# LRU gates placed inside the pair loop, 64x64 prompt scores, late scaling and a reordered start in a two-group encoder layer

## The chip, the cores and the metric

The kernel runs on one core of one Trainium2 chip. The metric is the device time in microseconds of one execution. Lower is better.

## What is computed

One layer of a streaming encoder, for 512 prompt tokens and 8 x 16 sample tokens that share all weights (`D` = 1024). Everything is float32. Cut to what matters here:

```python
def layer_forward(x, p, lb, cache, win_rows):
    x = x + 0.5 * swiglu(rms_norm(x, p['norm_ffn1']), p['w_ffn1_up'], p['w_ffn1_down'])   # D_FF = 2816
    m, st = mixer(rms_norm(x, p['norm_mix']), p, lb, cache, win_rows)
    x = x + m
    x = x + 0.5 * swiglu(rms_norm(x, p['norm_ffn2']), p['w_ffn2_up'], p['w_ffn2_down'])
    return x, st
# mixer: (aq, ak, av, hq, hf, hi, hg, lx, lg, ga, gb, gc) = split(h @ w_in)
#   A: attention, 16 heads in 4 groups, q and k normed per head; a prompt chunk of 64 queries
#      sees its own chunk and the two before it (192 keys); one learned sink per head
#   B: HGRN2, a gated linear recurrence
#   C: xc = conv4(lx);  r = sigmoid(xc @ lru_w_a + b_a);  ig = sigmoid(xc @ lru_w_x + b_x)
#      log_a = -8 * r * softplus(-lambda);  a = exp(log_a)
#      h_t = a_t * h_(t-1) + sqrt(1 - a_t^2) * ig_t * xc_t;   yc = h * gelu(lg)
#   merged = sigmoid(ga)*(ya@w_attn_o) + sigmoid(gb)*(yb@w_hgrn_o) + sigmoid(gc)*(yc@w_lru_o);  out = merged @ w_out
```

## The kernel before

**Layout.** Activations lie with features on the 128 partitions and the 640 tokens (512 prompt, then 128 sample) along the free axis, so x is eight tiles of 128x640. The matmul inputs are split into a high and a low part in a rounded float32 type (fp32r): `RA` and `RB` hold eight high tiles (0 to 7) and eight low tiles (8 to 15). `proj(w, r0, nk, c0, R)` makes one 128-column output tile of a weight: it loads the weight tile `wr` (512 KB, three buffers), makes `wh` and `wl` from it (lines 750 and 751), and issues for each of `nk` row blocks three products (wh x high, wh x low, wl x high) on two halves of 320 tokens, six matmuls a row block and 48 for eight. The result stands in two `pp` buffers of PSUM out of four, so that at most two projections are open. `scaled` moves it out, times the norm's factor `RS` (`late=False`), or copies it first and multiplies later (`late=True`).

**Order of the work.** The program is first recorded as a list of operations and then emitted by a planner, `Sched.run`, which keeps one in-order list for each engine. At each step it takes the operation that can start first by its own clock; among those that can start within 0.04 us of the earliest, the lowest priority number goes first. The priority is the number of the projection, `S.item`, plus `S.late`, or `S.item` less `lag` for loads and weight splits. Durations come from formulas: `dve(n)` is 0.066 + 1.042e-3 * n us, and `mm` has a `cost` for each kind of tile, with `RESIZE` = 0.1 us where the width of the output changes. Buffers come from tags (`pp` 4, `me` 2, `ml` 2 in PSUM; `wr`, `wh`, `wl`, `qq`, `lg`, `mgC` and more in SBUF), and the buffers of a tag are handed out strictly in program order. On the chip each engine follows its list and waits where an input isn't there.

**Stages,** with the stretches of the profiled span they fill:
- *Start (0 to 32 us).* `load_x` loads x in quarters (four prompt loads of 512 KB and four sample loads of 128 KB) through SP's queue; the first weight tile stands behind the first quarter. PE transposes each quarter, ACT and DVE copy it and split it into `RA`; ACT squares it for the first norm. `lag` in `load_x` orders the loads.
- *FFN 1 (to 470).* The hidden width is done in chunks of 4, 6, 6 and 6 tiles. The first chunk uses `proj`, the rest a Strassen-like scheme, `pair`, whose operands `combos` makes. Half of these are made by the function `rest()` that it returns, called ahead of the first chunk's down projections. *FFN 2 (1482 to the end)* is the same code with `sfx` "2". In FFN 1 the first two tiles are scaled late, in FFN 2 none.
- *Attention (470 to 700).* `qknorm` norms queries and keys; `query(m)` writes two heads (m of 8) as `qb`, 1024 columns, in which each head's block has zeros in the other head's rows. `prompt(m)` takes the 8 chunks of 64 queries in two halves `hh`, in each of which it makes two groups `i` of two chunks: one 128x128 by 64-to-192-column matmul for each chunk into a `me` buffer, a maximum (line 1064), exponentials, sums, then transposes (`pT`) and the product with the values (`pv_of`). `AHEAD` says how many gate or branch projections follow each m.
- *LRU (767 to 890).* `lru()` has a loop over four pairs of tiles: convolution of `branch(m)` (the first four are made in attention), two small projections with the block-diagonal weights `BH`/`BL` by `NH`/`NL`, exponentials, a scan along the tokens (line 1227), and the gate branch `LG`. Its end rows go to `CB` by copies that POOL or DVE may take. After the loop come five projections of the merge gate `GC`, `heads(0)` and `merge`.
- *HGRN2 (1010 to 1335)*, then `w_out` and FFN 2.

Of the kernel before, what the change touches and what calls it, by code (L numbers as in the profile page):

```python
# [345 lines left out]
def trunk_kernel(ctx: ExitStack, tc: tile.TileContext, A: dict, O: list):  # L346
# [122 lines left out]
    SK = fixed("SK", [P, 32])  # L469
    NAR = 13864  # L470
# [52 lines left out]
    in_region(RW, 2, [("qb", 1024, 2), ("pw", 1024, 2)])  # L523
# [23 lines left out]
    fill(EPSC.v, EPS, only=("DVE",))  # L547
    fill(ONEF[0:64, 64:128], 0.0, only=("DVE",))
# [195 lines left out]
    def proj(w, r0, nk, c0, R):  # L744
# [4 lines left out]
        dma(r, w[r0:r0 + nk * P, c0:c0 + P].rearrange("(k p) f -> p k f", p=P), lag=4)  # L749
        S.op([act(nk * P, lambda: nc.scalar.copy(h(), r())), dve(nk * P * 0.5, lambda: nc.vector.tensor_copy(h(), r()))], [r], [h], lag=2)  # L750
        S.op([dve(nk * P, lambda: nc.vector.tensor_tensor(l(), r(), h().bitcast(F32), op=ALU.subtract))], [r, h], [l], lag=1.5)  # L751
        ps = [S.buf("pp") for _ in range(2)]
        for k in range(nk):
            mm([(ps[i][:, :HT], a[:, k, :], R[:, o + k, i * HT:(i + 1) * HT].at(o + k), k == 0 and j == 0, k == nk - 1 and j == 2)
                for j, (a, o) in enumerate(((wh, 0), (wh, 8), (wl, 0))) for i in range(2)])
# [216 lines left out]
    def attention():  # L972
        ck, cv = A["cache_attn_k"][0], A["cache_attn_v"][0]
        sk = A["attn_sinks"][0].rearrange("(m two) -> two m", two=2)
        for h in range(2):
            dma(SK[h * 64:h * 64 + 64, 0:8].at(h), sk[h:h + 1, :].to_broadcast([64, 8]), after=(PRM.v,), small=True)
            for b in range(4):
                p0 = b * 32 + h * 16
                dma(SK[p0:p0 + 16, 8:16].at((b, h)), sk[h:h + 1, :].to_broadcast([16, 8]), after=(PRM.v,), small=True)
        S.op([dve(16, lambda: nc.vector.tensor_scalar(SK[:, 16:32](), SK[:, 0:16](), -1.0, None, op0=ALU.mult))], [SK.v, RS.v], [SK.v])  # L980
# [23 lines left out]
        for j in range(2):  # L1004
            q, r = qknorm(proj(W, 0, KD, AK + j * P, RA))
# [35 lines left out]
        def prompt(m, g, qb):  # L1041
            pT = S.buf("pT")
            for hh in range(2):
# [4 lines left out]
                for i in range(2):  # L1048
                    ps = S.buf("me")
                    calls = []  # L1050
                    for c in (2 * i, 2 * i + 1):
                        n = hh * 4 + c
                        w = min(n + 1, 3) * 64
                        o = (c % 2) * 192
                        e = 192 if c % 2 == 0 else 256
                        win[c] = ps[:, o:o + w], pw3[:, c, e - w:e].at(c)
                        calls.append((win[c][0], qb[:, n * P:(n + 1) * P], kd[g][:, (n + 1) * 64 - w:(n + 1) * 64], True, True))
                    mm(calls)
                    if hh == 0 and i == 0:
                        red = [(mx[:, c:c + 1].at(i), win[c][0]) for c in range(2)]  # L1060
# [5 lines left out]
                    ts(mi, mi, -0.125, ALU.mult, SK[:, 16 + m:17 + m], ALU.min, only=("DVE",))  # L1066
                    fn(ei, mi, AF.Exp, bias=SK[:, m:m + 1])
                    for c in (2 * i, 2 * i + 1):
                        fn(win[c][1], win[c][0], AF.Exp, scale=0.125, bias=mx[:, c:c + 1].at(i), accum=den[:, c:c + 1].at(i))
                    tt(di, di, ei, ALU.add, only=("DVE",))  # L1070
                    recip(di, di)
                    for c in (2 * i, 2 * i + 1):
                        ts(win[c][1], win[c][1], den[:, c:c + 1].at(i), ALU.mult)
# [8 lines left out]
            def pv_of(k, n):  # L1082

                src = pT[:, k * 512:k * 512 + n * 256].r("p (c h q) -> p c h q", h=2, q=64)
                mm([(po[h * 64:h * 64 + 64, k * P:(k + n) * P].r("p (c q) -> p c q", q=64), V[:, k, g, :], src[:, :, h, :], k == 0, k == 3)
                    for h in range(2)])
# [82 lines left out]
    def lru():  # L1169
        bds = [S.buf("bd") for _ in range(2)]  # L1170
        for b in bds:
            fill(b.v, 0.0)
        for j in range(4):
            xcs, rs, igs, las, lts = [], [], [], [], []
            for i in range(2):
# [16 lines left out]
                cp(CB[:, m, 0:3].at(m), y[:, TP - 3:TP], only=("POOL", "DVE"))  # L1192
                cp(CB[:, m, 3:27].at(m).r("p (b j) -> p b j", b=NB), smp(y.v)[:, :, SB - 3:], only=("POOL", "DVE"))
# [294 lines left out]
```

## Time and profile before

| | |
|---|---|
| median of 3 runs | 1921.0 us (1920.73 to 1923.34) |
| the profiled execution | 1923.28 us, span 1921.5 us, mean granted TensorE clock 0.996 |
| PE busy | 1898.9 us in 14654 instructions |
| PEld (weight loads beside PE) | 1853.0 us |
| DVE busy | 1389.1 us |
| ACT busy | 735.8 us |
| POOL busy | 44.3 us |
| HBM read and written | 143.32 and 10.63 MB |

Times are from the start of the span. A matmul's duration in the profile runs to the modelled end of its result, so a following matmul starts before it: the step from one start to the next says what an instruction costs in a stream, and busy time is the union of such spans. A float32 matmul call is two PE instructions in the profile, an fp32r one is one. `RA`, `RB` and the other names are the program's; most SBUF tiles outside them are slices of one tensor, `AR`, and are named so in the profile.

### The profile page before, as it was taken

What the parts mean: (1) busy time and instruction counts of PE and PEld (TensorE: products, weight loads), DVE (VectorE), ACT (ScalarE), POOL (GpSimd) and SP (SyncE); (2) the same over time, 40 slices, a digit from 0 to 9 for tenths busy, and PEclk for the clock granted to TensorE, in tenths of its full rate; (3) what the DMA queues carried; (4) which work ended last, traced back from release to release, by engine and by line L of the source; (5) the groups of instructions that cost most, each with busy time, mean ns of one, the idle gap of its engine ahead of it and who ended that gap; (6) DMA issues with size and microseconds to landing.
All of it is one profiled execution on the core that took longest, in us unless ns stands there. A gap on an engine that the chain in (4) does not pass through costs nothing.

```text
span 1921.5 us, 35215 instructions
## 1 busy us (share of the span) xinstructions
PE 1898.9 (99%) x14654; PEld 1853.0 (96%) x14654; DVE 1389.1 (72%) x2599; ACT 735.8 (38%) x1295; POOL 44.3 (2%) x86
## 2 busy tenths in 40 slices
PE   8999999999999999999999999999999999999999
PEld 8999999999999999999999999999999999999998
DVE  7897685877787773787547778877556978586784
ACT  6343251433478630876002344335112324142340
POOL 2000000000000000020000000000000000000000
PEclk9999999999999999999999999999999999999999
DMA  6232332224321212213222222222322133222322
GB/s 144 66 94 80 93 87 78 75 78 139 102 62 50 62 48 77 61 57 103 77 77 74 84 80 79 79 81 83 122 72 77 56 99 90 87 65 79 99 64 80
DMA packets 303488, 156.89 MB, mean 82 GB/s; under 512 B 21324, under 2 KB 300956, under 8 KB 303328
## 3 DMA queue, kind: packets, MB, share of 16 engines
q1 hardware_dynamic: 302576, 154.58, 27.7%
q8 instruction: 115, 1.88, 0.4%
q0 software_dynamic: 736, 0.06, 0.4%
q14 instruction: 45, 0.37, 0.1%
q10 hardware_dynamic: 16, 0.00, 0.0%
HBM read 143.32 MB, written 10.63 MB: 80 GB/s over the span
## 4 chain that ended last, share of the span: by engine, by line
PE 93%; DVE 4%; ACT 2%; issue 1%; DMA 1%; SPq 0%; ACTq 0%; DVEq 0%
PE pp L438 84%; PE me L438 4%; PE ml L438 3%; PE ml L447 1%; PE me L447 1%; DVE AR L383 1%; ACT AR L393 1%; DVE AR L369 1%; DVE RB L369 0%; DVE AR L1227 0%; ACT L393 0%; DMA RX<-in_x_prompt_dram 0%; DVE wl L751 0%; SPq L417 0%; DVE RA L369 0%
## 5 line engine op out<-in xcount | busy, mean ns | idle before, releaser
L438 PE MATMUL pp<-RA,wh 128*128 128x320 f32 x4192 | 815.0, 314 | 0.3 <-DVE AR L369 0.3
L438 PEld LDWEIGHTS pp<-RA,wh 128*128 128x128 f32 x4192 | 659.1, 189 | 13.1 <-issue 9.7
L438 PE MATMUL pp<-RA,wl 128*128 128x320 f32 x2096 | 490.7, 310 | 4.9 <-DVE wl L751 4.9
L438 PE MATMUL pp<-RB,wh 128*128 128x320 f32 x2016 | 389.0, 310 | 0.9 <-DVE AR L369 0.9
L438 PEld LDWEIGHTS pp<-RA,wl 128*128 128x128 f32 x2096 | 354.7, 188 | 5.9 <-DVE wl L751 5.9
L438 PEld LDWEIGHTS pp<-RB,wh 128*128 128x128 f32 x2016 | 320.4, 188 | 1.5 <-DVE AR L369 1.4
L750 DVE CAST wh<-wr 128x1024 fp32r<-128x1024 f32 (+2 forms) x142 | 89.4, 630 | 237.2 <-PE pp L438 236.5
L438 PE MATMUL pp<-RB,wl 128*128 128x320 f32 x1008 | 241.9, 310 | 1.6 <-DVE wl L751 1.6
L751 DVE TENSOR_TENSOR wl<-wr,wh 128x1024 fp32r<-128x1024 f32 (+2 forms) x196 | 216.7, 1106 | 1.6 <-ACT wh L750 1.0
L836 ACT CAST RW<-AR 128x512 fp32r<-128x512 f32 x180 | 110.4, 621 | 264.9 <-PE pp L438 135.0
L438 PEld LDWEIGHTS pp<-RB,wl 128*128 128x128 f32 x1008 | 172.1, 188 | 1.9 <-DVE wl L751 1.9
L369 DVE TENSOR_TENSOR AR<-AR 128x640 f32<-128x640 f32 (+12 forms) x272 | 140.0, 519 | 28.9 <-ACT AR L393 16.5
L369 DVE TENSOR_TENSOR AR<-pp,AR 128x320 f32<-128x320 f32 x268 | 127.6, 485 | 35.8 <-PE pp L438 32.7
L393 ACT ACTIVATE AR<-AR 128x640 f32<-128x640 f32 (+2 forms) x184 | 110.5, 604 | 96.9 <-DVE AR L369 89.6
L438 PE MATMUL pp<-RX,RW 128*128 128x320 f32 x864 | 138.6, 309 | 0.0
L438 PEld LDWEIGHTS pp<-RX,RW 128*128 128x128 f32 x864 | 129.6, 188 | 0.0
L833 DVE TENSOR_TENSOR RW<-AR,RW 128x512 fp32r<-128x512 f32 x180 | 122.3, 686 | 2.4 <-ACT RW L836 0.9
L393 ACT ACT_TABLE_LOAD x73 | 93.7, 1283 | 2.5 <-PEq L1476 1.4
L402 ACT COPY AR<-me 128x512 f32<-128x512 f32 (+3 forms) x72 | 25.8, 373 | 123.9 <-PE me L447 115.2
L383 DVE SCALAR_TENSOR_TENSOR AR<-pp,AR 128x320 f32<-128x320 f32 x128 | 61.3, 483 | 15.5 <-PE pp L438 15.4
L438 PE MATMUL pp<-RY,RW 128*128 128x320 f32 x432 | 69.2, 309 | 0.0
L750 ACT CAST wh<-wr 128x1024 fp32r<-128x1024 f32 (+1 forms) x54 | 53.7, 994 | 36.9 <-PE pp L438 36.5
(195 smaller groups left out, 1960.7 us busy)
## 6 DMA issues: line engine op xcount, KB each, us to landing
wr<-in_w_in_dram SPq DMA_DIRECT2D x84, 512.0 KB, 3.7
wr<-in_w_ffn_up_dram SPq DMA_DIRECT2D x52, 512.0 KB, 3.8
AR<-in_w_ffn_up_dram SPq DMA_DIRECT2D x36, 512.0 KB, 4.6
wr<-in_w_ffn_down_dram SPq DMA_DIRECT2D x48, 384.0 KB, 3.3
wr<-in_w_ffn_down_dram SPq DMA_DIRECT2D x16, 256.0 KB, 2.8
wr<-in_w_attn_o_dram SPq DMA_DIRECT2D x8, 512.0 KB, 3.7
AR<-in_state_hgrn_dram SPq DMA_DIRECT2D x8, 512.0 KB, 4.7
wr<-in_w_lru_o_dram SPq DMA_DIRECT2D x8, 512.0 KB, 3.8
```

The costliest lines, as they stand in the source:

```text
L369: alts = [dve(out.n, lambda: nc.vector.tensor_tensor(out(), a(), b(), op=op))]
L383: return S.op([dve(out.n, lambda: nc.vector.scalar_tensor_tensor(out(), a(), ap_of(s), b(), op0=op0, op1=op1), isinstance(s, View))], [a, ...
L393: nc.scalar.activation(out(), a(), func, bias=ap_of(bias), scale=ap_of(scale), **kw)
L402: alts = [act(out.n, lambda: nc.scalar.copy(out(), a()), 0, a), dve(out.n * (1.0 if a.in_psum else 0.5), lambda: nc.vector.tensor_copy(out ...
L438: nc.tensor.matmul(o(), l(), m(), start=s, stop=e)
L447: nc.tensor.transpose(o(), i(), d())
L750: S.op([act(nk * P, lambda: nc.scalar.copy(h(), r())), dve(nk * P * 0.5, lambda: nc.vector.tensor_copy(h(), r()))], [r], [h], lag=2)
L751: S.op([dve(nk * P, lambda: nc.vector.tensor_tensor(l(), r(), h().bitcast(F32), op=ALU.subtract))], [r, h], [l], lag=1.5)
L833: S.op([dve(out.n, lambda: nc.vector.tensor_tensor(out(), a(), b(), op=op))], [a, b], [out], lag=lag)
L836: S.op([act(out.n, lambda: nc.scalar.copy(out(), a()))], [a], [out], lag=lag)
```

## The change

- *Start:* 14 matmuls of 128x128 on the constant `ONEF` are recorded ahead of x. The first weight tile is loaded and split in four pieces of two row blocks, each ordered behind a quarter of x by its lag; the lags of x's quarters change a little.
- *FFN:* `rest()` gets `S.late` = 4. In FFN 2 the first tile is now scaled late.
- *Attention:* `qb` is a plain 512 columns, written by one operation over all partitions. The scores of a half `hh` are one group of eight calls on 64x64 tiles: for each chunk and head a tile with 64 rows and 64 output partitions, placed so that two chunks fill all four quarters of the array; even chunks go to one `me` buffer and odd ones to the other. For odd chunks the heads stand in swapped halves, for which the sinks `SK` get swapped copies and `pv_of` reads other columns. The key projections are scaled late.
- *LRU:* one of the `GC` gates is projected inside each of the four pairs and the fifth after them. The planner's duration of the scan is doubled. The copies into `CB` go to ACT or DVE.
- *HGRN2:* the copies of the 16-blocks go to ACT or DVE.

```diff
@@ mm, cost
+            if l.proto.shape[0] == 64 and w == 64:
+                return max(0.054, 0.42e-3 * m.n)
@@ buffers
-    SK = fixed("SK", [P, 32])
+    SK = fixed("SK", [P, 48])
-    in_region(RW, 2, [("qb", 1024, 2), ("pw", 1024, 2)])
+    in_region(RW, 2, [("qb", 512, 2), ("pw", 1024, 2)])
@@ start
+    warm = S.buf("me")
+    mm([(warm[:, i % 4 * P:(i % 4 + 1) * P], ONEF.v, ONEF.v, True, True) for i in range(14)])
@@ load_x
-            lag = (12, 2.7, 2.6, 2.5)[c]
+            lag = (12, 2.7, 2.65, 2.6)[c]
@@ proj
-    def proj(w, r0, nk, c0, R):
+    def proj(w, r0, nk, c0, R, slices=None):
...
+        if slices is not None:
+            for k in range(0, nk, 2):
+                rk, hk, lk = (b[:, k:k + 2, :].at(k) for b in (wr, wh, wl))
+                dma(rk, src[:, k:k + 2, :], lag=slices[k // 2])
+                cp(hk, rk, only=("ACT", "DVE"))
+                tt(lk, rk, hk.cast(F32), ALU.subtract)
@@ ffn
-                    late = not sfx and f < 2
-                    g = scaled("fA" + sfx, proj(wu, 0, KD, f * P, R), late)
+                    late = f < (1 if sfx else 2)
+                    g = scaled("fA" + sfx, proj(wu, 0, KD, f * P, R, (13, 3.69, 3.64, 3.59) if not sfx and f == 0 else None), late)
...
             if f0 == 0:
+                S.late = 4.0
                 rest()
+                S.late = 0.0
@@ attention
+            dma(SK[64 - h * 64:128 - h * 64, 32:40].at((h, 8)), sk[h:h + 1, :].to_broadcast([64, 8]), after=(PRM.v,), small=True)
...
-        for b in qbs + qss + pws:
+        for b in qss + pws:
             fill(b.v, 0.0, only=("POOL",))
...
-            q, r = qknorm(proj(W, 0, KD, AK + j * P, RA))
+            q, r = qknorm(proj(W, 0, KD, AK + j * P, RA), True)
@@ prompt
-                for i in range(2):
-                    ps = S.buf("me")
-                    calls = []
-                    for c in (2 * i, 2 * i + 1):
...
-                        calls.append((win[c][0], qb[:, n * P:(n + 1) * P], kd[g][:, (n + 1) * 64 - w:(n + 1) * 64], True, True))
-                    mm(calls)
+                pss, calls = [S.buf("me") for _ in range(2)], []
+                for c in range(4):
...
+                    o = (c // 2) * 192
+                    win[c] = pss[c % 2][:, o:o + w], pw3[:, c, e - w:e].at(c)
+                    for f in range(2):
+                        a, b = f * 64, (f ^ (c % 2)) * 64
+                        calls.append((win[c][0][a:a + 64, :], qb[b:b + 64, n * 64:(n + 1) * 64], kd[g][b:b + 64, (n + 1) * 64 - w:(n + 1) * 64],
+                                      True, True))
+                mm(calls)
@@ query
+            stt(qb.v, q[:, 0:TP], prm(QN), r[:, 0:TP], ALU.mult, ALU.mult)
             for h in range(2):
-                stt(qb[a:b, :].at(h).r("p (n h q) -> p n h q", n=8, h=2)[:, :, h, :], q[a:b, 0:TP].r("p (n q) -> p n q", n=8), prm(QN, a, b),
-                    r[a:b, 0:TP].r("p (n q) -> p n q", n=8), ALU.mult, ALU.mult)
@@ lru
+        gates, more = [], lambda m: gate(GC, m, "mgC")
...
-                cp(CB[:, m, 0:3].at(m), y[:, TP - 3:TP], only=("POOL", "DVE"))
+                cp(CB[:, m, 0:3].at(m), y[:, TP - 3:TP], only=("ACT", "DVE"))
...
-                S.op([dve(T, lambda o=hs.v, a=a.v, t=t.v: nc.vector.tensor_tensor_scan(o(), a(), t(), 0.0, op0=ALU.mult, op1=ALU.add))],
+                S.op([dve(2 * T, lambda o=hs.v, a=a.v, t=t.v: nc.vector.tensor_tensor_scan(o(), a(), t(), 0.0, op0=ALU.mult, op1=ALU.add))],
...
                 parts(RB, m, g.v)
+                if i == 0:
+                    gates.append(more(len(gates)))
...
-        more = lambda m: gate(GC, m, "mgC")
-        gates = [more(m) for m in range(5)]
+        while len(gates) < 5:
+            gates.append(more(len(gates)))
@@ hgrn
-                            cp(a4[p, :, p].at(j), atc[p, :].r("p (t l) -> p t l", t=NT), only=("ACT", "POOL"))
+                            cp(a4[p, :, p].at(j), atc[p, :].r("p (t l) -> p t l", t=NT), only=("ACT", "DVE"))
```

More of the change, by code (lines that the diff above doesn't have):

```diff
@@ L979, in attention @@
                 dma(SK[p0:p0 + 16, 8:16].at((b, h)), sk[h:h + 1, :].to_broadcast([16, 8]), after=(PRM.v,), small=True)
-        S.op([dve(16, lambda: nc.vector.tensor_scalar(SK[:, 16:32](), SK[:, 0:16](), -1.0, None, op0=ALU.mult))], [SK.v, RS.v], [SK.v])
+        for o, c, n in ((16, 0, 16), (40, 32, 8)):
+            S.op([dve(16, lambda o=o, c=c, n=n: nc.vector.tensor_scalar(SK[:, o:o + n](), SK[:, c:c + n](), -1.0, None, op0=ALU.mult))],
+                 [SK.v, RS.v], [SK.v])
         ms = S.buf("ms")
@@ L993, in attention, with qknorm @@
         qbs, qss, pws = ([S.buf(t) for _ in range(2)] for t in ("qb", "qs", "pw"))
-        for b in qbs + qss + pws:
+        for b in qss + pws:
             fill(b.v, 0.0, only=("POOL",))
-        def qknorm(ps):
-            q, s, r, u = scaled("qq", ps), S.buf("qt"), S.buf("qr"), S.buf("qu")
+        def qknorm(ps, late=False):
+            q, s, r, u = scaled("qq", ps, late), S.buf("qt"), S.buf("qr"), S.buf("qu")
             rnorm(q, s, r, u, bd64, 64)
@@ L1047, in prompt @@
                 win = {}
-                for i in range(2):
-                    ps = S.buf("me")
-                    calls = []
-                    for c in (2 * i, 2 * i + 1):
[L1052 to L1056, printed above, removed]
-                        calls.append((win[c][0], qb[:, n * P:(n + 1) * P], kd[g][:, (n + 1) * 64 - w:(n + 1) * 64], True, True))
-                    mm(calls)
-                    if hh == 0 and i == 0:
-                        red = [(mx[:, c:c + 1].at(i), win[c][0]) for c in range(2)]
+                pss, calls = [S.buf("me") for _ in range(2)], []
+                for c in range(4):
+                    n = hh * 4 + c
+                    w = min(n + 1, 3) * 64
+                    o = (c // 2) * 192
+                    e = 192 if c % 2 == 0 else 256
+                    win[c] = pss[c % 2][:, o:o + w], pw3[:, c, e - w:e].at(c)
[4 more added lines that the diff above has]
+                mm(calls)
+                for i, ps in enumerate(pss):
+                    cols = [(2 * i, win[i]), (2 * i + 1, win[i + 2])]
+                    if hh == 0:
+                        red = [(mx[:, c:c + 1].at(i), v[0]) for c, v in cols]
                     else:
@@ L1065, in prompt @@
                     mi, di, ei = (x[:, 2 * i:2 * i + 2].at(i) for x in (mx, den, es))
[L1066 to L1069, printed above, removed]
+                    pos, neg = ((0, 16), (32, 40))[i]
+                    ts(mi, mi, -0.125, ALU.mult, SK[:, neg + m:neg + m + 1], ALU.min, only=("DVE",))
+                    fn(ei, mi, AF.Exp, bias=SK[:, pos + m:pos + m + 1])
+                    for c, v in cols:
+                        fn(v[1], v[0], AF.Exp, scale=0.125, bias=mx[:, c:c + 1].at(i), accum=den[:, c:c + 1].at(i))
                     tt(di, di, ei, ALU.add, only=("DVE",))
                     recip(di, di)
-                    for c in (2 * i, 2 * i + 1):
-                        ts(win[c][1], win[c][1], den[:, c:c + 1].at(i), ALU.mult)
+                    for c, v in cols:
+                        ts(v[1], v[1], den[:, c:c + 1].at(i), ALU.mult)
                 for i in range(2):
@@ L1082, in pv_of @@
             def pv_of(k, n):
-                src = pT[:, k * 512:k * 512 + n * 256].r("p (c h q) -> p c h q", h=2, q=64)
-                mm([(po[h * 64:h * 64 + 64, k * P:(k + n) * P].r("p (c q) -> p c q", q=64), V[:, k, g, :], src[:, :, h, :], k == 0, k == 3)
-                    for h in range(2)])
+                src = pT[:, k * 512:k * 512 + n * 256].r("p (t x q) -> p t x q", x=4, q=64)
+                mm([(po[h * 64:h * 64 + 64, k * P:(k + n) * P].r("p (t e q) -> p t e q", e=2, q=64), V[:, k, g, :],
+                     src[:, :, 1:3, :] if h else src[:, :, 0:4:3, :], k == 0, k == 3) for h in range(2)])
             for k, n in ((0, 2), (2, 2), (1, 2), (3, 1)):
@@ L1191, in lru @@
                     stt(smp(xc.v)[:, :, :s], hist, w, smp(xc.v)[:, :, :s], ALU.mult, ALU.add)
-                cp(CB[:, m, 0:3].at(m), y[:, TP - 3:TP], only=("POOL", "DVE"))
-                cp(CB[:, m, 3:27].at(m).r("p (b j) -> p b j", b=NB), smp(y.v)[:, :, SB - 3:], only=("POOL", "DVE"))
+                cp(CB[:, m, 0:3].at(m), y[:, TP - 3:TP], only=("ACT", "DVE"))
+                cp(CB[:, m, 3:27].at(m).r("p (b j) -> p b j", b=NB), smp(y.v)[:, :, SB - 3:], only=("ACT", "DVE"))
                 r, ig = S.buf("lr"), S.buf("li")
@@ L1226, in lru @@
                 hs = rs[i]
-                S.op([dve(T, lambda o=hs.v, a=a.v, t=t.v: nc.vector.tensor_tensor_scan(o(), a(), t(), 0.0, op0=ALU.mult, op1=ALU.add))],
+                S.op([dve(2 * T, lambda o=hs.v, a=a.v, t=t.v: nc.vector.tensor_tensor_scan(o(), a(), t(), 0.0, op0=ALU.mult, op1=ALU.add))],
                      [a.v, t.v], [hs.v])
-                cp(CB[:, m, 27:28].at(m), hs[:, TP - 1:TP], only=("POOL", "DVE"))
-                cp(CB[:, m, 28:36].at(m), smp(hs.v)[:, :, SB - 1], only=("POOL", "DVE"))
+                cp(CB[:, m, 27:28].at(m), hs[:, TP - 1:TP], only=("ACT", "DVE"))
+                cp(CB[:, m, 28:36].at(m), smp(hs.v)[:, :, SB - 1], only=("ACT", "DVE"))
                 hss.append(hs)
```

12 lines of the change are left out of this document (7 added, 5 removed).

## The prediction, made before the change was run

> **What bounds the kernel now.** I read the mean clock first (0.996 on the one core), then the first part of the page, then PE's list of waits, then windows of the stages, then the timeline at each stall.
>
> PE is busy 1898.9 us of a span of 1921.5, so nearly everything that isn't PE is already covered. Time can come from two places only: PE's own instructions, and the stretches in which PE waits or runs below its full pace. The second kind is found by counting matmuls in windows. In the first fence the columns are the window, its length, busy time with instructions in brackets for PE, PEld, DVE, ACT and POOL, then the granted clock. The row 144 to 192 is the full pace: 329 matmuls in 48 us, 6.854 per us or 0.146 us each. A window with fewer has lost the difference, through idle time or a low clock.
>
> ```profile
> core 0: us, PE busy (x) PEld busy (x) DVE busy (x) ACT busy (x) POOL busy (x), PEclk, DMA share, GB/s
> 9.45:14.50 5.05, 5.01 (x21) 5.04 (x22) 3.54 (x6) 4.12 (x12) 4.23 (x8) 1.00 1.13 323
> 76.00:90.00 14.00, 12.41 (x73) 11.99 (x72) 12.64 (x35) 3.15 (x5) 0.00 (x0) 0.88 0.20 57
> 144.00:192.00 48.00, 48.00 (x329) 48.00 (x328) 35.12 (x61) 16.85 (x29) 0.00 (x0) 1.00 0.28 81
> 513.00:700.00 187.00, 186.45 (x1520) 172.37 (x1519) 149.64 (x416) 133.95 (x338) 1.28 (x6) 1.00 0.21 57
> 788.00:800.00 12.00, 9.22 (x45) 8.33 (x44) 12.00 (x21) 9.46 (x13) 3.72 (x4) 0.74 0.11 31
> 820.00:830.00 10.00, 7.62 (x52) 7.36 (x51) 10.00 (x19) 3.41 (x5) 4.05 (x6) 1.00 0.22 64
> 1486.00:1500.00 14.00, 13.11 (x88) 12.63 (x87) 12.55 (x20) 2.15 (x3) 0.00 (x0) 1.00 0.13 39
> 1532.00:1550.00 18.00, 16.28 (x100) 15.88 (x99) 12.85 (x25) 1.47 (x3) 0.00 (x0) 0.91 0.20 58
> ```
>
> The waits say what PE stood for; columns are total us, times, longest.
>
> ```profile
> PE pp L438 <- DVE wl L751: 6.4, 5, 2.4
> PE me L447 <- DMA RX<-in_x_prompt_dram: 4.6, 2, 2.6
> PE me L438 <- DVE NL L369: 2.4, 1, 2.4
> PE ml L447 <- DMA AR<-in_norm_ffn_dram: 2.3, 1, 2.3
> PE pp L438 <- DVE AR L369: 1.2, 2, 0.9
> ```
>
> The reader is to see that each wait is for a small DVE operation standing behind others in DVE's queue, or for x at the start. In attention (513 to 700) PE loses only 0.55 us of 187: there the PE instructions themselves must go.
>
> **The change part by part.**
>
> *Prompt scores.* Before, each head pair m issues 8 calls of 128x128 weights, half of the query block being zeros; each call is two PE instructions. After: 16 calls of 64x64 on the four quarters of the array.
>
> ```profile
> 514.45 0.45 PE L438 MATMUL pp<-RA,wl 128*128 128x320 f32 x2
> 514.74 0.81 PE L438 MATMUL me<-AR,RW 128*128 128x192 f32 x4
> 515.26 0.88 PE L438 MATMUL pp<-RA,wh 128*128 128x320 f32 x4
> ...
> L438 PE MATMUL me<-AR,RW 128*128 128x192 f32 x96 | 19.6, 331 | 0.0
> ...
> L438 PE MATMUL ml<-AR 128*64 128x256 f32 x96 | 12.1, 388 | 0.0
> ...
> L438 PE MATMUL me<-AR 128*32 128x128 f32 x128 | 5.2, 279 | 0.0
> ```
>
> A group of four instructions of 192 columns holds PE from 514.74 to 515.26, 0.52 us, and the projection behind it needs 0.88 for its first four instead of the usual 0.75, 0.13 more: 0.65 us, so 163 ns per instruction. Per m there are three such groups and one of 64 and 128 columns, which I estimate from this at 0.55: 2.5 us, and 20.0 us for the eight m.
> After, what one instruction costs depends on how many quarters work at once. The trace has no 64x64 tile, but it has halves and strips. The 64-wide weights (x96, eight groups of twelve) take 12.1/8 = 1.51 us a group; less the 0.39 of the last one, starts are 1.12/11 = 102 ns apart, half of the 217 that 256 columns would take alone at 163 per 192: two at once. The 32-wide ones (x128, eight groups of 16) are (0.65 - 0.28)/15 = 25 ns apart against 109 alone: four at once. Both ways of cutting the array run at their full number, so I take four at once: 41 ns for 192 columns, and 27 ns for the short ones, estimated at the closest starts just found. Per m: 24 x 0.041 + 8 x 0.027 = 1.2 us, plus two groups (not four) that each pay 0.13 on return and 0.1 for the change of width, the planner's own constant: 1.66. Eight m: 13.3 us. Gain 6.7, say 7.0, as some old groups also stood apart by small gaps. Upper end 10 (20.0 less bare 1.2 x 8).
> A rule of the Trainium skill speaks against this. "TensorEngine Tiling (Array Packing)", Gotcha 1, says that different row tiles cannot use one PSUM bank at the same time, and here the first two calls (rows 0 to 63 and rows 64 to 127) write two halves of one bank. By that rule only two quarters would overlap and the sum would end at 1909.9; no run so far shows two row tiles on one bank, so it stands as a rival below.
> With two at once the scores cost 24 x 0.082 + 8 x 0.054 + 0.46 = 2.86 per m, 22.9 in all: 2.9 worse than now. That is the lower end.
> Beside it: one query operation over 128 partitions replaces two over 64, the zero fills go, and the first half's reductions become two in each bank; by the planner's 0.066 us start that is under 0.6 us of DVE in all, hidden, as DVE is busy 149.64 and ACT 133.95 of 187. If that cover were gone it would cost the 0.6. The scores now wait for both `me` buffers; see the rivals. The value matmuls only read other columns: 0. Two more small POOL loads of the sinks stand 500 us ahead of their use: 0.
>
> *Rest of the Strassen operands, `S.late = 4.0`, in both FFNs.*
>
> ```profile
> 77.50 0.82 DVE L369 TENSOR_TENSOR RW<-RW 128x640 f32<-128x640 f32 x1
> 78.23 0.68 DVE L751 TENSOR_TENSOR wl<-wr,wh 128x512 fp32r<-128x512 f32 x1
> ...
> 78.97 0.56 PE L438 MATMUL pp<-RB,wl 128*128 128x320 f32 x2 [1.59 <-DVE wl L751]
> ```
>
> The weight's low part waits on DVE behind 0.82 us operations of `rest()`; PE idles 1.59 us and then runs at a low clock. The window 76 to 90 lost 96 - 73 = 23 matmuls, 3.4 us; its twin in FFN 2 (1532 to 1550) 123.4 - 100 = 23.4, also 3.4. Moved back four items, rest goes behind the down projections' weights. Late next are the first products of `pair`, which need the same operands some 28 us later; DVE has about 1.4 us free in 14 there, so I take 2.6 of 3.4 in each. Ends: 3.4, and -2 if about half of rest's ten DVE steps still stand before the first product and the 3.4 stays lost in part.
> On the clock: 1.59 us idle was enough for a clock of 0.88 over 14 us. "TensorE: Matmul & The Clock Gate", Part 1 of the Trainium skill, puts the fall to half clock after an idle window of about 3.4 us. By that rule only the idling itself, 1.6 and 1.7 us, would come back and the sum would end at 1901.9; the trace shows more lost, and it decides.
>
> *FFN 2's first tiles late-scaled.* PE waited 0.9 us (the list's last row) because the four `pp` buffers were held until the norm came; 1486 to 1500 lost 96 - 88 = 8 matmuls, 1.2 us. Copies empty the buffers instead. Take 1.0; ends 1.2 and -0.5, since DVE at 12.55 of 14 takes two more multiplications. *K projections late:* the same list row holds another 0.3; take 0.3, ends 0.3 and -0.3.
>
> *LRU.* Before, the pair loop has only LG and branch projections to give PE, and the five gates come after.
>
> ```profile
> 791.00 1.48 DVE L1227 TENSOR_TENSOR_SCAN AR<-AR 128x640 f32<-128x640 f32 x1
> 792.40 1.53 DVE L369 TENSOR_TENSOR AR<-AR 128x640 f32<-128x640 f32 x2
> 793.85 0.81 DVE L369 TENSOR_TENSOR NL<-AR,NH 128x640 fp32r<-128x640 f32 x1
> ...
> 794.72 0.64 PE L438 MATMUL me<-NL,BH 128*128 128x320 f32 x1 [2.41 <-DVE NL L369]
> ```
>
> PE waits 2.41 us for NL, which stands behind scans that take 1.48 us where the planner's formula, 0.066 + 1.042e-3 x 640, says 0.73; doubling the count in that formula gives 1.40. Windows 788 to 800 and 820 to 830 lost 82.2 - 45 and 68.5 - 52 matmuls: 5.4 and 2.4, together 7.8 us. One gate per pair gives PE 48 x 0.146 = 7.0 us of work each, moved from after the loop, where PE has no gap to lose. Its own cost is two DVE scalings and a weight split per gate in a stage where DVE is full in places (12.00 of 12), and small copies (POOL 3.72 us for four) move to ACT or DVE. I take 6.0 of 7.8; ends 7.8 plus 1 for smaller waits, and 2. The same move of copies in HGRN: 0, no wait of PE there.
>
> *Start.*
>
> ```profile
> 1.77 0.43 SPq L417 DMA_DIRECT2D wr<-in_w_ffn_up_dram  x1
> ...
> 4.49 1.97 PE L447 MATMUL me<-ident,RX 128*128 128x128 f32 x8 [1.95 <-DMA RX<-in_x_prompt_dram]
> ...
> 17.15 1.04 PE L447 MATMUL me<-ident,RX 128*128 128x128 f32 x8
> ```
>
> The same eight instructions take 1.97 us at 4.49 and 1.04 at 17.15: PE starts slow, and does 21 instructions in 5.05 us before 14.5. From then on it is continuous. Warm it would save about half of 5.0; and with three quarters of the weight tile (393 KB) behind later quarters of x, x's second quarter comes 393 KB / 323 GB/s = 1.2 us sooner: upper end 3.7. Against it: 14 warm-up calls at 1.97/4 = 0.49 less drain, about 0.44 us, are 6.2 us if all run slow; from 1.2 us they end at 7.4, past x at 4.49, and the memset behind them on DVE holds the copies of x; SP issues three more DMAs of 0.43 us before x's last quarter. Lower end -1.5. I take 1.5, nearer the middle, as both rows bear on it.
>
> **Sum:** 7.0 + 2.6 + 2.6 + 1.0 + 0.3 + 6.0 + 1.5 = 21.0 us. The profiled execution took 1923.28 us (span 1921.5), 2.3 over the median of 1921.0; 21.0 off it is 1902.3, and off the median 1900.0, which I forecast.
>
> **The rivals.**
> *Two quarters at once.* The scores give -2.9 instead of 7.0: 1900.0 + 9.9 = 1909.9. For it: half-array rows show two; against: the strips show four.
> *DVE is the limit, so its stalls move.* Rest gives 0 in both FFNs and LRU 2.5: 1900.0 + 5.2 + 3.5 = 1908.7. For it: DVE is full in 788 to 800 and 12.64 of 14 after 76; against: 35.12 of 48 soon after, so DVE can catch up.
> *Both of these:* 1918.6, no measurable change.
> *Slower: PE idles for the second `me` buffer.* Each of the 16 score groups now needs both buffers free, hence the last exponentials of the group before; PE is in order, and if no projection is placed there it stands. It turns the forecast into a loss from (21.0 + 3.8)/16 = 1.55 us per group; at 1.8 it gives 1928.8. For it: ACT is 72% busy (133.95 of 187). Against: PE lost 0.55 us in the whole stage, so projections fill the waits today.
>
> **How the numbers follow.** Forecast 0.60, DVE limit 0.18, two quarters 0.11, both 0.05, slower 0.06. A measurement here can tell about 0.2%, 3.8 us, from no change: faster 0.89, same 0.05, slower 0.06. Upper ends added give 30.8, so 1890 is the low bound; the high bound takes in both single rivals and some more of the lower ends: 1914, leaving out 0.11.
>
> **What would show it.** Right: score instructions of 64x64 about 41 ns apart and the `me` scores' busy time near half; no wait of PE on wl at 77 and 1535; matmul counts of the LRU windows at 6.85 per us; clock at 1.00 after 76. Wrong: 80 ns between score starts; a new PE wait on the first `pair` product; PE idle ahead of `me` in attention; x's first transposes at 7 us with nothing won by 24 us.

## The result, and the profile after

| | before | after |
|---|---|---|
| median | 1921.43 us (1920.73 to 1923.34) | 1900.22 us (1900.11 to 1900.37) |
| ratio to before | | 0.9888, 95% interval 0.9871 to 0.9905 |
| profiled execution, and its span | 1923.28, 1921.5 us | 1900.11, 1897.8 us |
| mean granted clock | 0.996 | 1.00 |

The change takes 21.2 us off the median, and the forecast was 1900.0. A second set of the same kernel gave 1899.83 us. By stage not every term held, though, and that is what the experiments are about.

Two lines of the page after: the busy times, and the shares of the chain that ended last.

```profile
PE 1887.5 (99%) x14810; PEld 1837.6 (97%) x14810; DVE 1385.5 (73%) x2609; ACT 755.9 (40%) x1342; POOL 19.9 (1%) x44
...
PE 98%; DVE 1%; ACT 0%; issue 0%; DVEq 0%
```

PE's busy time fell by 11.4 us and the span by 23.7, so about half of what the span lost is idle time of PE; the other half is in its instructions, stretches at a low clock included. In the kernel before the same chain read PE 93%, DVE 4%, ACT 2%. PE's waits after:

```profile
PE pp L440 <- DVE AR L383: 1.9, 4, 0.6
PE pp L440 <- ACT RA L393: 1.1, 2, 0.8
PE me L440 <- DVE EPSC L412: 1.1, 1, 1.1
PE pp L440 <- DVE RA L383: 0.7, 2, 0.4
```

The waits on `wl`, x and `NL` are gone. New is a set of short ones, the longest after the start 0.8 us; L383 adds a down projection's result to x and so empties its `pp` buffer. Windows after, with the columns of the prediction's windows (from 790 on, those of 10 us in which before had lost matmuls):

```profile
76.00:90.00 14.00, 12.91 (x85) 12.15 (x84) 13.24 (x41) 1.93 (x3) 0.00 (x0) 1.00 0.21 61
144.00:192.00 48.00, 48.00 (x330) 48.00 (x329) 33.71 (x58) 14.83 (x25) 0.00 (x0) 1.00 0.26 73
508.00:700.00 192.00, 192.00 (x1718) 173.19 (x1717) 149.89 (x412) 138.59 (x343) 0.62 (x2) 1.00 0.22 59
1486.00:1500.00 14.00, 14.00 (x98) 14.00 (x97) 13.62 (x21) 4.32 (x6) 0.00 (x0) 1.00 0.08 22
1505.00:1530.00 25.00, 23.84 (x159) 23.08 (x158) 19.46 (x35) 5.73 (x9) 0.00 (x0) 1.00 0.25 73
790.00:800.00 10.00, 10.00 (x70) 10.00 (x70) 6.54 (x11) 9.00 (x13) 0.00 (x0) 1.00 0.21 59
800.00:810.00 10.00, 10.00 (x69) 9.79 (x68) 5.60 (x12) 9.83 (x14) 0.00 (x0) 1.00 0.24 68
...
820.00:830.00 10.00, 10.00 (x70) 10.00 (x69) 10.00 (x25) 4.12 (x7) 0.00 (x0) 1.00 0.26 76
...
860.00:870.00 10.00, 10.00 (x70) 10.00 (x70) 10.00 (x24) 5.70 (x8) 0.00 (x0) 1.00 0.29 85
```

The reader is to see three things. The full pace is unchanged (330 matmuls in 48 us). The LRU windows are at full pace although DVE is still full in two of them. And 76 to 90 has 85 of the 96 matmuls it could have: a loss of 11 is left there, with the clock at 1.00, and of 12 in 1505 to 1530 (171 possible, 159 done).

*Where the time came from.* First or last starts of the same matmuls in both traces give the gain at points along the span.

| marker | before | after | gained so far | in this stretch |
|---|---|---|---|---|
| first down projection (`pp<-RB,wh`) | 73.9 | 72.2 | 1.7 | start 1.7 |
| first `pair` product (`pp<-RX,RW`) | 108.3 | 104.9 | 3.4 | rest of FFN 1: 1.7 |
| first norm of the mixer (`NH,ones`) | 462.9 | 459.5 | 3.4 | 0 |
| first LRU product (`me<-NH,BH`) | 766.9 | 755.8 | 11.1 | attention: 7.7 |
| first HGRN matmul (`me<-RY,AR`) | 1012.7 | 991.7 | 21.0 | LRU: 9.9 |
| last norm (`NH,ones`) | 1481.5 | 1460.5 | 21.0 | HGRN, `w_out`: 0 |
| first FFN 2 product `pp<-RB,RW` | 1572.2 | 1548.1 | 24.1 | front of FFN 2: 3.1 |
| the last of them | 1869.5 | 1845.4 | 24.1 | 0 |

On each side of the LRU marker both kernels do the same number of `pp` matmuls (1484 from the first norm of the mixer, 1496 to HGRN), so its two rows can be compared. Four of the views behind the table, of before and of after (count, shortest, middle and longest duration in ns, first and last start):

```profile
L438 PE MATMUL me<-NH,BH x32: 306/309/632, 766.9 to 879.0; 128*128 128x320 f32 x32
L438 PE MATMUL me<-RY,AR x1408: 182/183/270, 1012.7 to 1320.9; 128*32 128x16 f32 x152, 128*32 128x32 f32 x16, 128*64 128x64 f32 x8
```

```profile
L440 PE MATMUL me<-NH,BH x32: 304/308/418, 755.8 to 881.6; 128*128 128x320 f32 x32
L440 PE MATMUL me<-RY,AR x1408: 182/183/270, 991.7 to 1299.9; 128*32 128x16 f32 x152, 128*32 128x32 f32 x16, 128*64 128x64 f32 x8
```

### The profile page after: what moved, and what is told of

The parts are those of the page before. It is cut to its first block, busy times and chain, and to the rows that moved or that the text cites. A ratio compares the mean times of both kernels' runs of the same rounds, so it can differ in the third digit from the quotient of the medians.

```text
span 1897.8 us, 35531 instructions
## 1 busy us (share of the span) xinstructions
PE 1887.5 (99%) x14810; PEld 1837.6 (97%) x14810; DVE 1385.5 (73%) x2609; ACT 755.9 (40%) x1342; POOL 19.9 (1%) x44
## 4 chain that ended last, share of the span: by engine, by line
PE 98%; DVE 1%; ACT 0%; issue 0%; DVEq 0%
PE pp L440 88%; PE me L440 4%; PE ml L440 3%; PE ml L449 1%; PE me L449 1%; DVE RB L369 0%; DVE RA L369 0%; ACT RA L393 0%; ACT AR L402 0%; DVE AR L369 0%; DVE wl L764 0%; DVE RW L369 0%; DVE RA L383 0%; DVE AR L403 0%; DVE wh L763 0%
## 5 line engine op out<-in xcount | busy, mean ns | idle before, releaser
L763 DVE CAST wh<-wr 128x1024 fp32r<-128x1024 f32 (+2 forms) x131 | 82.9, 633 | 218.6 <-PE pp L440 218.3
L369 DVE TENSOR_TENSOR AR<-AR 128x640 f32<-128x640 f32 (+12 forms) x272 | 140.0, 519 | 31.3 <-ACT AR L393 23.2
L763 ACT CAST wh<-wr 128x1024 fp32r<-128x1024 f32 (+2 forms) x64 | 62.5, 976 | 74.9 <-PE pp L440 70.9
L383 DVE SCALAR_TENSOR_TENSOR AR<-pp,AR 128x320 f32<-128x320 f32 x128 | 61.1, 483 | 15.5 <-PE pp L440 15.4
```

The source lines that it names most:

```text
L369: alts = [dve(out.n, lambda: nc.vector.tensor_tensor(out(), a(), b(), op=op))]
L383: return S.op([dve(out.n, lambda: nc.vector.scalar_tensor_tensor(out(), a(), ap_of(s), b(), op0=op0, op1=op1), isinstance(s, View))], [a, ...
```

## The experiments

"Less" and "more" compare medians. All runs stood beside a kernel before of 1921.2 to 1922.3 us; the changed kernel gave 1900.22 and 1899.83, so differences under about 1 us between sets are at the edge of what can be told.

### The scores: taken back, and alone

The first kernel is the changed one with the old scores, `qb`, `SK` and `pv_of`; the second is the kernel before with only the new ones.

```diff
-                pss, calls = [S.buf("me") for _ in range(2)], []
-                for c in range(4):
+                for i in range(2):
+                    ps = S.buf("me")
+                    calls = []
+                    for c in (2 * i, 2 * i + 1):
...
```

> The changed kernel with the old prompt scores (128x128 tiles, zero-padded query block, two groups a half); the rest of the change stays. Theory A (each part of the change acts by itself, and the scores are worth what their instructions save): the trace after shows a 16-instruction group of 192 columns holding PE 0.81 us plus 0.10 before and 0.10 behind it, against 2 x 0.65 before, and 0.9 against 1.2 for the shorter half, so 0.6 us per m and 4.7 in all: 1904.9 us. The prediction's own term says 7.0: 1907.2. Theory B (the order in attention matters more than the instructions): over 9 us, above 1909, with PE idle or far more changes between number formats in attention.

> The kernel before with only the 64x64 prompt scores of the change. Theory A: 4.7 us less than before, about 1916.7 us; the prediction's term: 7.0 less, 1914.4; Theory B (order): gains of 9 or more, or a loss where PE waits for both me buffers, which was the slower rival (above 1921).

Without the new scores: 1906.99 us (1906.23 to 1907.38), 6.8 more than after. Alone in the kernel before: 1914.89 (1913.75 to 1915.85), ratio 0.9961 [0.9946, 0.9976], 7.4 less than the 1922.28 beside it. Both bear out the prediction's 7.0, though the interval of the second runs from 4.6 to 10.4 us; by its trace the stretch from the mixer's first norm to the first LRU product is 7.1 us shorter than before (304.01 and 296.96 us). The timeline of PE in the changed kernel, start, duration, operation:

```profile
516.89 0.46 PE L440 MATMUL pp<-RA,wl 128*128 128x320 f32 x2
517.28 0.88 PE L440 MATMUL me<-AR,RW 64*64 64x192 f32 x16
518.09 0.85 PE L440 MATMUL pp<-RA,wh 128*128 128x320 f32 x4
```

Its costliest groups have this line (busy us, mean ns of one), where before had 19.6 busy for 96:

```profile
L440 PE MATMUL me<-AR,RW 64*64 64x192 f32 x192 | 11.9, 331 | 0.0
```

Sixteen instructions take 0.88 us to the end of the last, which itself lasts 0.33: starts are 0.55/15 = 37 ns apart, 163/37 = 4.4 times as close as the full array's. So all four quarters worked at once. By the rule of the Trainium skill that the prediction weighed ("TensorEngine Tiling (Array Packing)", Gotcha 1) two row tiles on one bank would have stood 82 ns apart; here the two write different halves of the partitions of the bank, and the trace does not agree with the rule for that case.

One new group holds PE from 517.28 to 518.09, 0.81 us, with 0.10 of a gap ahead of it and 0.10 more for the projection behind: 1.01 against 2 x 0.65 for the two groups it replaces. Sixteen times 0.29 is 4.7, less than the 7 us measured, because it rests on one group of each kind. Added up over the stretch, from each start to the next, the score instructions take 17.9 us in the kernel before and 12.1 with the new ones alone, 5.7 less; the `pp<-RA,wh` matmuls, which stand behind most groups, take 113.9 and 112.3, 1.6 less; all others together 0.3 more. Split the same way, the prediction's sum holds 15.8 less 11.2, or 4.6, for the scores and 16 returns of 0.13, or 2.1, for the projections. The transposes behind the scores (`ml<-ident,RW`) stand in fewer groups (17 for 29), but take 0.7 us more themselves.

The slower rival named PE standing for the second `me` buffer. Attention shows 192.00 busy of 192: no such wait.

### The gates: taken back, and alone

```diff
-        gates, more = [], lambda m: gate(GC, m, "mgC")
...
-                if i == 0:
-                    gates.append(more(len(gates)))
...
-        while len(gates) < 5:
-            gates.append(more(len(gates)))
+        more = lambda m: gate(GC, m, "mgC")
+        gates = [more(m) for m in range(5)]
```

> The changed kernel with the five GC gates projected after the pair loop again; scan price and copies stay as changed. Theory A (the gates fill PE's gaps in the LRU loop): the windows of the LRU stage lose 6 to 9 us of matmuls again, about 1907 to 1909 us. Theory C (the scan's true price in the planner did it): at most 1.5 us lost, below 1901.7.

> The kernel before with one thing changed: the merge gates are projected inside the pair loop; scan price, copies and all else stay as before. Theory G (the gates alone fill what PE lost between 750 and 900, 9.4 us of matmuls): 9 to 11 us less than the kernel before, so about 1911, and every window of 10 us from 790 to 870 holds 66 to 72 matmuls. Theory C (gates, scan price and the copies taken off POOL only work together, since the small copies on POOL or a scan behind its due time still hold NL): 4 to 6 us less, about 1916, with a wait of PE on NL or BH left of over 1 us.

With the gates after the loop again: 1911.63 us (1911.42 to 1913.81), 11.4 more than after, and more than either theory allowed (theory A ended at 1909). Three of its windows, and two of its waits:

```profile
780.00:790.00 10.00, 7.07 (x36) 6.18 (x35) 10.00 (x16) 7.78 (x15) 0.00 (x0) 0.83 0.18 52
810.00:820.00 10.00, 7.27 (x40) 7.01 (x39) 10.00 (x23) 3.56 (x6) 0.00 (x0) 0.83 0.36 105
850.00:860.00 10.00, 8.70 (x55) 7.75 (x53) 9.63 (x21) 6.10 (x10) 0.00 (x0) 1.00 0.19 54
```

```profile
PE pp L440 <- DVE wl L764: 3.2, 2, 2.7
PE me L440 <- DVE NL L369: 2.9, 2, 2.4
```

Against 70 each these windows lack 34, 30 and 15 matmuls, 79 x 0.146 = 11.5 us, which is about the whole difference. The gates alone in the kernel before: 1913.61 us (1910.94 to 1914.44), ratio 0.9957 [0.9945, 0.9970], 7.6 less than the 1921.19 beside it. By time that lies between its two theories. The trace has the signs of theory G (66 to 70 matmuls in every window of 10 us, and a wait on `NL` of 0.4 us, not over 1) with a smaller gain: its windows from 790 to 890 hold 66 to 70 matmuls, eleven short of ten times 70 in all, so 1.6 us are still lost, and HGRN starts 1012.7 - 1004.1 = 8.6 us earlier, of which 0.8 was there at the first `pair` product (107.5 against 108.3). So the gates by themselves are worth 7.8 us there, with the scan's price and the copies as before.

### The scan's price

```diff
-                S.op([dve(2 * T, lambda o=hs.v, a=a.v, t=t.v: nc.vector.tensor_tensor_scan(...
+                S.op([dve(T, lambda o=hs.v, a=a.v, t=t.v: nc.vector.tensor_tensor_scan(...
```

> The changed kernel with the planner's old duration of the scan (0.73 us instead of 1.40); gates stay in the loop. Theory A: the gates cover what DVE is late by, so 1900 to 1901.5 us. Theory C: the loss of the LRU stage comes back, 3 us or more, above 1903.

1901.52 us (1900.79 to 1902.19), 1.3 more than after and at the edge of theory A, with waits on `NL` of 0.4 and on an ACT result of 0.3 back. So the price is worth about a microsecond once the gates are in the loop. The copies that moved off POOL were not undone by themselves.

### The rest of the operands: early again, and later still

```diff
-                S.late = 4.0      (second kernel: 6.0)
                 rest()
-                S.late = 0.0
```

> The changed kernel with rest() at its old priority in both FFNs. The prediction's terms say 2 x 2.6 lost, 1905.4 us. Theory D (DVE is nearly the limit there, so part of the stall only moved to the emptying of the down projections' buffers): by the markers 1.7 in FFN 1 and about 1.9 in FFN 2 lost, 1903.8, and the wait on wl at about 75 us back with a clock under 1.00 behind it.

> The changed kernel with S.late = 6 instead of 4 for the rest of the operands in both FFNs. Theory D (DVE is what limits 70 to 90 and 1505 to 1530, whatever the order): within 0.6 us of the unaltered kernel of this call, with the waits of PE on L383 still 1 to 2 us. Theory O (order decides; the operands still stand ahead of the emptying of pp): 1 to 2 us less, and the waits on L383 under 0.5 in all; if the operands then come too late, a new wait on the first pair product (RX,RW) at 105 to 110.

Early again: 1901.56 us (1900.24 to 1902.51), only 1.3 more than after, where the prediction had 5.2 for the two FFNs and theory D 3.6. Its four executions fall in two pairs: 1900.24 and 1900.70 with a mean granted clock of 1.000, 1902.42 and 1902.51 with 0.999. The trace is that of 1902.42, so it shows one of the dearer two. Its windows, and PE at both stalls:

```profile
76.00:90.00 14.00, 12.29 (x83) 11.94 (x82) 13.42 (x43) 1.45 (x2) 0.00 (x0) 1.00 0.25 75
1505.00:1530.00 25.00, 23.14 (x148) 22.88 (x147) 18.56 (x33) 5.96 (x9) 0.00 (x0) 0.93 0.19 54
```

```profile
77.92 0.56 PE L440 MATMUL pp<-RB,wl 128*128 128x320 f32 x2 [1.71 <-DVE wl L764]
...
1515.28 0.71 PE L440 MATMUL pp<-RA,wl 128*128 128x320 f32 x2 [1.86 <-DVE wl L764]
1515.79 1.27 PE L440 MATMUL pp<-RA,wh 128*128 128x320 f32 x4
```

The old stall on `wl` is back (1.71 us at 77.9), but this window does 83 matmuls, two fewer than after. With the change part of the idling stayed (14 - 12.91 = 1.09 us, against 1.59 before), in pieces. After, PE at the same place, and DVE ahead of it:

```profile
80.23 0.42 PE L440 MATMUL pp<-RB,wh 128*128 128x320 f32 x1 [0.41 <-DVE AR L383]
81.23 0.71 PE L440 MATMUL pp<-RB,wh 128*128 128x320 f32 x3 [0.58 <-DVE AR L383]
```

```profile
73.27 0.68 DVE L764 TENSOR_TENSOR wl<-wr,wh 128x512 fp32r<-128x512 f32 x1
...
74.27 0.81 DVE L369 TENSOR_TENSOR RA<-AR,RA 128x640 fp32r<-128x640 f32 x1
...
75.74 0.81 DVE L369 TENSOR_TENSOR RA<-RW,RA 128x640 fp32r<-128x640 f32 x1
76.48 0.81 DVE L369 TENSOR_TENSOR RW<-RW 128x640 f32<-128x640 f32 x1
...
78.55 0.81 DVE L369 TENSOR_TENSOR RA<-RW,RA 128x640 fp32r<-128x640 f32 x1
...
79.70 0.48 DVE L383 SCALAR_TENSOR_TENSOR AR<-pp,AR 128x320 f32<-128x320 f32 x1
80.10 0.67 DVE L764 TENSOR_TENSOR wl<-wr,wh 128x512 fp32r<-128x512 f32 x1
```

PE now stands for the emptying of `pp`. The writes of `RA` and the `RW<-RW` step are `rest()`'s: against the kernel with `rest()` early, one weight's low part (73.27) moved ahead of the last four of its ten steps, but these four still run ahead of the first emptying (79.70) and of the next low part (80.10). So `rest()` did not go behind the down projections' weights, as the prediction had it. What separates the kernel before from the changed one with `rest()` early is the clock. In FFN 1 the 1.71 us idle left it at 1.00 here, while the kernel before, after 1.59 us, had 0.88 and did 73; in FFN 2 the 1.86 us here was followed by 0.93, four matmuls taking 1.27 us instead of 0.75, and the window lost 11 matmuls (148 against 159).

Later still (6 items): 1899.88 us (1899.50 to 1900.72) beside 1899.83 for the unaltered kernel, with L383's waits still 1.9 us. This decides nothing between its two theories: by the traces the lists of DVE (2609 instructions), ACT (1342), PE (14810) and POOL are the same, one by one, as in the unaltered kernel, so the run is a repetition of it. That fits the planner's rule, by which the priority chooses only among operations that can start within 0.04 us of each other. Whether DVE is the limit there, or only the order, stays open. In FFN 1 DVE has no gap over 0.1 us from 68.1 to 87.9 us after, which speaks for the limit; in FFN 2 it stands idle for 2.0, 1.7 and 1.7 us between 1519.6 and 1528.7, right behind the short waits and some 20 us before the first product of `rest()`'s operands there (`pp<-RB,RW`, 1548.1), so there was room on DVE for its steps later.

### Late scaling in FFN 2

```diff
-                    late = f < (1 if sfx else 2)
+                    late = not sfx and f < 2
```

> The changed kernel with FFN 2's first tile scaled at once again. The prediction's term says 1.0 lost, 1901.2 us, with a PE wait of 0.9 us on the scaling. Theory D: DVE, full in the stretch behind it, takes the gain back, so under 0.4 lost, below 1900.6.

1901.24 us (1900.60 to 1901.57), 1.0 more than after, and this wait is back:

```profile
PE pp L440 <- DVE AR L369: 0.9, 1, 0.9
```

That is the prediction's 1.0, at the edge of what can be told by the time, but plain in the trace. The late scaling of the key projections was not undone by itself.

### The start: without the warm-up, without the pieces, without both

```diff
-    warm = S.buf("me")
-    mm([(warm[:, i % 4 * P:(i % 4 + 1) * P], ONEF.v, ONEF.v, True, True) for i in range(14)])
...
-            lag = (12, 2.7, 2.65, 2.6)[c]
+            lag = (12, 2.7, 2.6, 2.5)[c]
...
-                    g = scaled("fA" + sfx, proj(wu, 0, KD, f * P, R, (13, 3.69, 3.64, 3.59) if not sfx and f == 0 else None), late)
+                    g = scaled("fA" + sfx, proj(wu, 0, KD, f * P, R), late)
```

> The changed kernel without the 14 warm-up matmuls; the four weight pieces and the lags stay. The first down projection starts at 72.2 us after and 73.9 before, so the whole start is worth 1.7 us. Theory W (the clock is what the start wins): without the block the first 5 us of x work run slow again, 1.5 to 2.5 us lost, 1901.7 to 1902.7. Theory S (the order of the loads wins it): at most 0.5 lost, below 1900.8. Theory L (the block costs, as x's first transposes begin at 6.67 instead of 4.49): up to 1 us won, 1899.2 to 1900.

> The changed kernel with the first weight tile loaded and split whole, with the old lags of x; the warm-up block stays. Theory W: at most 0.5 us lost, below 1900.8. Theory S: 1.5 us or more lost, above 1901.7, with PE waiting for x's second quarter as before (2.6 us).

> The changed kernel without either part of the start: no warm-up block, and the first weight tile in one load with one split, as before. Theory S (the start is worth the 1.7 us that the first down projection came earlier): 1901.9, first RB,wh matmul at 73.9. Theory N (each part alone cost under 1 us to undo because PE is filled later from what it has anyway): under 0.7 us over the unaltered kernel of this call, with the first RB,wh matmul later by over 1 us but the last RB,RW matmul by under 1.

| | median | span of the profiled execution | first down projection |
|---|---|---|---|
| after | 1900.22, 1899.83 | 1897.8, 1897.9 | 72.2, 72.3 |
| no warm-up | 1899.93 (1899.64 to 1901.24) | 1898.9 | 73.2 |
| no pieces | 1900.92 (1900.48 to 1901.71) | 1899.1 | 73.9 |
| neither | 1900.90 (1899.92 to 1901.56) | 1898.9 | 73.7 |

Without the warm-up the time shows nothing (theories S and L both allow that, theory W does not). Without the pieces it is 0.7 to 1.1 us longer, between theories W and S, with a wait for x of 1.1 us, not 2.6; without both it is as long as without the pieces (1.1 over 1899.83, 1.0 in span), between theories S and N. The marker itself moves: in the eight traces that have both parts of the start the first down projection begins at 71.6 to 72.8, in the four with neither at 73.1 to 73.9. The means, 72.2 and 73.6, put the whole start at about 1.4 us. PE at the start, after, and then without the warm-up:

```profile
1.06 5.53 PE L440 MATMUL me<-onef 128*128 128x128 f32 x28 [1.06 <-DVE EPSC L412]
6.52 0.23 PE L449 MATMUL ml<-ident,AR 8*128 8x8 f32 x1
6.67 1.09 PE L449 MATMUL me<-ident,RX 128*128 128x128 f32 x8
```

```profile
4.34 1.97 PE L449 MATMUL me<-ident,RX 128*128 128x128 f32 x8 [1.79 <-DMA RX<-in_x_prompt_dram]
```

The block does what the prediction feared and what it hoped for: x's first transposes start 2.3 us later, behind 28 instructions at 0.20 us each, and then take 1.09 us instead of 1.97. The transposes of x's fourth quarter start at 15.43 after, 16.67 without the warm-up and 17.15 before, so in these traces the block has won 1.2 us by then; the median does not show it. The sign of being wrong that the prediction named, transposes at 7 us with nothing won by 24, came only in its first half. The profile's granted clock reads 1.00 over the whole of this stretch, before as well (2 to 24 us), where the same eight instructions take 1.97 us at 4.49 and 1.04 at 17.15: that column does not show this slowness.

### The changed kernel once more

> The changed kernel once more, unaltered, beside the three below, so that differences of about 1 us are taken on one chip. Both theories: 1900.2, within 0.5; span 1897.8, clock 1.00.

1899.83 us (1899.30 to 1900.22), ratio 0.9889 [0.9876, 0.9903], span 1897.9.

## Why the prediction was right, and where it was not

*The total* was right: 21.0 forecast, 21.2 between medians. Part of that is luck. Against the profiled execution, from which the terms were worked out, the gain was 1923.28 - 1900.11 = 23.2, so the sum was 2.2 short; the forecast was read off the median, and the profiled execution of before lies 1.9 over that. The choice of the median was sound for a reason that the prediction did not know: that execution had lost more to the clock than most. Its mean granted clock is 0.996; of the 23 runs of before beside the experiments one has that, all others 0.997 or 0.998. In the kernel with only the gates, the stall of FFN 2 is the same to 0.01 us, and yet what follows differs.

```profile
1536.72 0.56 PE L438 MATMUL pp<-RA,wl 128*128 128x320 f32 x2 [1.72 <-DVE wl L751]
```

```profile
1528.00 0.56 PE L438 MATMUL pp<-RA,wl 128*128 128x320 f32 x2 [1.71 <-DVE wl L751]
```

```profile
1522.00:1540.00 18.00, 16.30 (x111) 15.89 (x110) 14.39 (x28) 2.26 (x4) 0.00 (x0) 1.00 0.20 59
```

The first is before, whose window 1532 to 1550 stands in the prediction; the other two are the gates alone (PE's timeline, then the window of 18 us around the stall): the same wait, the clock at 0.91 and at 1.00, 100 and 111 matmuls, 1.6 us. So a stall of this length costs 1.7 us in one execution and 3.3 in another. Within one kernel the same is seen, as far as the mean clock tells, in the pairs of `rest()` early and in the gates alone, which took 1910.94 and 1911.17 us at a mean clock of 0.999 and 1913.61 to 1914.44 at 0.998. This also fits the runs of before, spread over 1919.5 to 1923.5 in these sets, while those of after lie within 1.1.

*Scores, 7.0:* right (6.8 and 7.4), and so was the step behind it, that starts would be 41 ns apart (37), and about so its two parts (5.7 and 1.6, for 4.6 and 2.1). The busy time of the wide ones fell to 11.9 of 19.6, not near half. The rival with two at once is excluded.

*LRU, 6.0:* too small. This is the step that failed most. The prediction counted two windows (7.8 us) and took 6.0 of them; from 750 to 900 the trace of before held three more short ones (from 800, 830 and 860 here):

```profile
790.00:800.00 10.00, 7.22 (x31) 6.33 (x30) 10.00 (x17) 7.49 (x11) 3.72 (x4) 0.69 0.12 35
800.00:810.00 10.00, 10.00 (x68) 10.00 (x68) 6.46 (x13) 8.66 (x13) 0.00 (x0) 0.97 0.27 76
...
820.00:830.00 10.00, 7.62 (x52) 7.36 (x51) 10.00 (x19) 3.41 (x5) 4.05 (x6) 1.00 0.22 64
830.00:840.00 10.00, 9.94 (x67) 9.47 (x66) 6.63 (x17) 7.58 (x12) 0.00 (x0) 1.00 0.32 95
...
860.00:870.00 10.00, 9.55 (x63) 8.87 (x62) 10.00 (x20) 6.05 (x8) 3.62 (x5) 1.00 0.18 52
```

Against the 70 of their neighbours these five lack 39, 2, 18, 3 and 7: 69 matmuls, at 70 in 10 us 9.9 us, and after the change all of them but one are there. The LRU marker gives the same 9.9. Of the 3.9 that the term fell short, 1.8 are what it left out of its 7.8, 1.7 the three windows that it did not count (12 matmuls), and the rest the pace, 0.146 us a matmul where this stage has 0.143. The gates alone brought 7.8; the scan's price, worth 1.3 when undone, is over half of what is missing, and the copies were not undone by themselves. The reason for taking less than all, that DVE is full in places, was wrong: DVE is still full in 820 to 830 after, but PE has the gate to do meanwhile.

*Rest, 5.2:* too large. The markers give 1.7 in FFN 1 and 3.1 - 1.0 = 2.1 in FFN 2, 3.8 in all, and undoing it costs 1.3 us in median and 2.3 in the span of the profiled execution, one of the dearer pair. The step that failed is "rest goes behind the down projections' weights": the last four of its steps stayed ahead of them, and 11 and 12 matmuls are still lost where 23 each were. Whether DVE's "about 1.4 us free in 14" would have been enough was not tried, as no kernel here has `rest()` later than that. The rival "DVE is the limit, so its stalls move" is wrong for the LRU; for the FFNs the stalls did move in part, and the reason is open. The signs named for this step, no wait on `wl` and a clock of 1.00, came true; what the prediction did not name, a new wait on L383, is where the rest of the gain went. By the rule of the Trainium skill that the prediction weighed ("TensorE: Matmul & The Clock Gate", Part 1) only the idling itself would have come back, 1.6 and 1.7 us. That is near the size measured, but for another reason: the clock did fall, after idles of 1.6 to 2.4 us and not 3.4, though not after each of them, and it was part of the idling that stayed.

*Late scaling, 1.0:* right. *Start, 1.5:* about right, 1.7 by the marker in this pair, 1.4 between the means of all traces, and 1.0 to 1.4 by undoing both parts. *HGRN, 0:* right, 21.0 gained before and behind it. *The slower rival:* no wait of PE for a `me` buffer in attention.

The stretches of the profiled pair give 1.7 (start), 1.7 (rest in FFN 1), 7.7 (scores and late keys), 9.9 (LRU) and 3.1 (rest in FFN 2 and late scaling), 24.1, less 0.4 at the end of the span, which I did not trace. The errors of LRU (3.9 too small) and rest (1.4 too large) partly cancelled, which is luck too. Undoing the parts one by one gives 6.8, 11.4, 1.3 (scan), 1.3, 1.0 and 1.1, 22.9 with the scan. Undoing the gates costs 1.5 more than before had lost without them (11.4 against 9.9); two of its windows have a clock of 0.83, but in before one had 0.69, and the reason stays open.

## What to carry to other kernels

Count matmuls in equal windows over a whole stage, not only at the two worst stalls: on an engine that is the bound, what lay outside those two was 12 of the 69 matmuls that the stage had lost. Where one engine waits for another that is full, giving the waiting engine work of its own to do meanwhile can take the loss away, as the gates did here with all but one of the 69. Before a run with another priority is read as a test of the order, see in the trace that the order changed. A sum worked out from one profiled execution is to be checked against the spread of the other runs before it is trusted to 2 us.

## What was not expected of the hardware

- All four quarters of the array ran at once on two banks of PSUM, with row tiles that share a bank in different partition halves: 37 ns between starts of 192 columns, where the full array needs 163.
- The clock fell, or did not, after one and the same wait: 0.91 after 1.72 us, 1.00 after 1.71; 0.88 after 1.59 in one kernel and 1.00 after 1.71 in another. In one and the same execution, before, the wait of 2.41 us that ended at 794.72 was followed by 0.50 from 795 to 799, and the one in the line below by 1.00. The Trainium skill ("TensorE: Matmul & The Clock Gate", Part 1) says that the activity window runs freely, so that the point of transition depends on where in it the work falls; that is in keeping with the variation here, though not with a need for 3.4 us of idling. Waits up to 0.8 us never lowered it in the kernel after.

```profile
825.37 0.56 PE L438 MATMUL pp<-RA,wl 128*128 128x320 f32 x2 [2.38 <-DVE wl L751]
```

- Warming the array won nothing that the median shows where the wait for the data is short: 28 instructions took from 1.06 to 6.59, and the transposes behind them won 0.9 us and started 2.3 later; 1899.93 us without the block, 1900.22 and 1899.83 with it.
